# Both heads of a pair in one reduction over the partitions, pool sums behind it, and weights two column tiles ahead

## The chip, the cores and the metric

The kernel runs on one core of a Trainium2 chip. The metric is the device time of one execution in microseconds; of the kernel before, three runs are known: 1245.39, 1246.07 and 1249.59, median 1246.07. The engines of the core are TensorE (PE in the rows, with its weight loads as PEld), VectorE (DVE), ScalarE (ACT), GpSimd (POOL) and SyncE (SP), which here issues every transfer. Each engine works through its own queue in order and waits at the head of it until what it needs is there.

## The reference

Two layers of an encoder on 1024 prompt tokens and 32 sample tokens, all in fp32, width 1024.

- Layer 0: RMSNorm, one input projection to 3072 columns, which are split into `u`, `q`, `k`, `v`, `g_pool`, `g_att` of 512 each. The pooling branch takes trailing means of `u` over windows of 2, 4, 8 and 16 tokens (one window for each group of 128 channels), subtracts the token, and maps each group by a 128x128 matrix. The attention branch has 8 heads of 64 channels; a query sees its own chunk of 64 tokens and the 8 chunks before it, with a learned bias by clipped distance, and a softmax over the keys:

```
s = where(key_chunk >= 0, q @ k.T * 64**-0.5 + bias, -inf)
p = softmax(s, axis=-1);  o = p @ v
```

  Both branches are multiplied by SiLU gates, concatenated, and go through an output projection, RMSNorm and a residual.
- Layer 1: RMSNorm, a projection to 5128 columns, an mLSTM mixer with 4 heads of 256 channels in chunks, gates, an output projection, RMSNorm and a residual. The change reaches it only through the number of buffers.

## The kernel before, in words

Activations lie transposed, channels on the partitions and the 1056 tokens along the free dimension, in three token groups of 384, 384 and 288. Each projection is computed in column tiles of 128. A weight tile is split into a rounded part `wh` and a residue `wl`, the activations likewise, and three products give fp32 accuracy: per column tile and token group that is 24 matmuls (`mm3`, lines 107 to 109), called a dense step here. `load_w` fetches a weight tile in two halves into `wr` (two buffers), ScalarE casts them to `wh` (line 94), and VectorE or GpSimd subtracts to get `wl` (line 95). `wh` and `wl` have two buffers each, so the next tile is loaded while one is in use.

Layer 0 runs over four pairs of heads. Dense steps that belong to later work (a next `q`, `v`, `u` or gate tile, by the table PLAN) are put on a list, and `fill()` takes the next step from it wherever attention would leave TensorE without work; `fill_all()` takes the rest ahead of the next pair. `take()` hands out the loaded weight tile and starts the load of the next one.

Attention of a pair is done for each head `e` in two halves `hf` of 512 queries, keys on the partitions. `att_s` computes scores (lines 353 and 354: two matmuls for each key block, into `ps`), adds the bias while evacuating to `st` (VectorE at 363, ScalarE at 371), takes the elementwise maximum over the key blocks on VectorE into `mx` (380 to 387), and lets GpSimd take the maximum over the partitions into `mb` (389). `power` subtracts `mb` (396, VectorE) and takes the exponential (397, ScalarE). `att_pv` multiplies by the values (407), `att_take` copies the result out of PSUM into `ro` and `rg` (415, 416), and `att_out` divides (429, 430, VectorE), multiplies by the gate (431, GpSimd) and stores. `st` has four buffers; a head's first half takes one of them, its second half two. `ro`, `rg` and the PSUM tile `pv` have one buffer each. The order for a pair is: scores of both first halves, two fills, exponentials of head 0, scores of head 0's second half, a fill, exponentials of head 1, values of the first halves, scores of head 1's second half, values of head 0's second half, the sample's values (`values`, line 484), two fills with head 1's exponentials between them, values of head 1's second half. Each `att_s` issues a reduction of its own; the sample has a small one (464).

The pooling branch: once the last step of a `u` tile is through, `pool_sums` adds shifted copies on GpSimd (line 512: one addition for window 2, up to four for window 16). `finish` (519, 521, VectorE) is put on a list `due` and runs two fills later; the pooling matmul `pool_mix` (534) runs right after the gate tile's last step.

`out_proj` reads the mixed activations back through `xr` (two buffers) and projects them; the evacuation of its tiles is at lines 759 to 763.

The code fixes the order of the program, but the engines' queues are put in order by a planner that simulates a timeline ahead of the run (`schedule_with_timeline_sim=True`): an instruction that it deems ready can come ahead of an earlier one that it deems not ready. `issue_after(x)` keeps an instruction behind `x` on its engine.

Of the kernel before, what the change touches and what calls it, by code (L numbers as in the profile page):

```python
# [33 lines left out]
class Net:  # L34
# [43 lines left out]
    def load_w(self, src, keep=None, eng=None, parts=False):  # L78
        nc = self.nc
        eng = eng or nc.vector  # L80
        if isinstance(keep, tuple):
            wh, wl = keep
        elif keep is None:
            wh = self.wp.tile([128, 8, 128], F32R, name="wh")
            wl = self.wp.tile([128, 8, 128], F32R, name="wl")
        else:
            wh = self.lp.tile([128, 8, 128], F32R, name=f"wh{keep}")
            wl = self.lp.tile([128, 8, 128], F32R, name=f"wl{keep}")

        def part(i):  # L90
            k = slice(4 * i, 4 * i + 4)
            wr = self.wp.tile([128, 4, 128], F32, name="wr", bufs=2)
            self.wdma = nc.sync.dma_start(out=wr, in_=src[:, k]).ins
            nc.scalar.copy(out=wh[:, k], in_=wr)  # L94
            eng.tensor_tensor(out=wl[:, k], in0=wr, in1=wh[:, k].bitcast(F32), op=ALU.subtract)  # L95
        if parts:
            return (wh, wl), [lambda: part(0), lambda: part(1)]
        part(0)
        part(1)
        return wh, wl  # L100
# [229 lines left out]

    def att_s(self, pr, e, hf, Q, KA, KB, B):
        nc = self.nc
# [6 lines left out]
        for group in banks:  # L339
# [3 lines left out]
            for js in group:  # L343
# [32 lines left out]
                off += w  # L376
        mx = self.lp.tile([128, 512], F32, name="mx", bufs=2)
        if hf == 0:
# [6 lines left out]
        for j in rest:  # L385
            dst, a, b = place[j]
            nc.vector.tensor_tensor(out=mx[:, a - q0:b - q0], in0=mx[:, a - q0:b - q0], in1=dst, op=ALU.max)
        mb = self.lp.tile([128, 512], F32, name="mb", bufs=2)
        nc.gpsimd.partition_all_reduce(mb, mx, 128, bass_isa.ReduceOp.max)  # L389

# [109 lines left out]
    def pool_sums(self, g, u):  # L500
# [8 lines left out]
        while sh < w:  # L509
            dst = tmp[:, i % 2]  # L510
            lo += sh
            nc.gpsimd.tensor_tensor(out=dst[:, lo:L], in0=src[:, lo:L], in1=src[:, lo - sh:L - sh], op=ALU.add)
            src = dst
            sh *= 2
            i += 1

        def finish():
            with self.tc.issue_after(self.ev):
                nc.vector.tensor_tensor(out=src[:, 15:15 + w - 1], in0=src[:, 15:15 + w - 1], in1=self.cnt[:, g, :w - 1], op=ALU.mult)
                for a, n in ((15, SEQ), (30 + SEQ, DEC)):  # L520
                    nc.vector.scalar_tensor_tensor(out=u[:, a:a + n], in0=src[:, a:a + n], scalar=1.0 / w, in1=u[:, a:a + n],
                                                   op0=ALU.mult, op1=ALU.subtract)
        self.due.append([2, finish])

# [15 lines left out]
    def layer0(self):  # L540
# [13 lines left out]
        def take(want):  # L554
            assert seq[nxt[0]] == want
            if not self.wq:
                self.wq.append(self.load_w(w0[want]))
            nxt[0] += 1
            if nxt[0] < len(seq):
                self.wq.append(self.load_w(w0[seq[nxt[0]]], None, self.weng))  # L560
            return self.wq.pop(0)
# [102 lines left out]
        def do_gp(g):  # L664
            def make():
                pools["gp", g] = self.lq.tile([128, T], F32, name="gp", bufs=1)
                return self.gated(pools["gp", g])
            self.later(lambda: take(GP + g), xs, make, lambda: self.pool_mix(g, pools["u", g], pools["gp", g]))

        for pr in range(NPAIR):  # L670
# [19 lines left out]

            def S(e, hf):
                return self.att_s(pr, e, hf, Q, KA, KB, B)
            scores()
            p00, w00 = S(0, 0)
            p10, w10 = S(1, 0)
            self.fill(2)
            w00()
            p01, w01 = S(0, 1)
            self.fill()
            w10()  # L700
            power()
            od = self.att_new()
            self.att_pv(0, 0, p00, vt, od)
            self.fill()
            w01()
            self.att_pv(1, 0, p10, vt, od)
            self.att_out(pr, od, 0, 512, gate)
            p11, w11 = S(1, 1)
            self.fill()
            od = self.att_new()  # L710
            self.att_pv(0, 1, p01, vt, od)
            values()
            self.fill()
            w11()
            self.fill()
            turn()
            self.att_pv(1, 1, p11, vt, od)
# [8 lines left out]
    def out_proj(self, wsrc, gpost, late, resid, finish, ytiles=(), nx0=4, nopen=2, end=False, w2=2, anchor=None):  # L726
# [7 lines left out]
        for gi in range(3):  # L734
            s, n = GR[gi]
            x = self.new_x(gi)
            for k in early + list(late):
                if k in late:
                    src = late[k][:, s:s + n]
                else:  # L740
                    xr = self.tp.tile([128, 384], F32, name="xr", bufs=2)
                    with tc.issue_after(wdma) if gi and 1 else nullcontext():
                        nc.sync.dma_start(out=xr[:, :n], in_=mv[:, k, s:s + n])
                    src = xr[:, :n]
                with tc.issue_after(anchor) if gi and anchor is not None else nullcontext():
                    self.split_x(x, k, src, None, nc.gpsimd if gi < 2 and k % 2 == 0 else None)
# [71 lines left out]
    def gate_weights(self):  # L818
        nc, wp = self.nc, self.wp
        wr = wp.tile([128, 8, 64], F32, name="wr", bufs=2)  # L820
        nc.sync.dma_start(out=wr, in_=self.io["w1g"])
        wh = wp.tile([128, 8, 128], F32R, name="wh")
        nc.scalar.copy(out=wh[:, :, 0:64], in_=wr)
# [455 lines left out]
```

## Time and profile before

| | |
|---|---|
| median of three runs | 1246.07 us |
| the profiled execution's own time | 1249.51 us |
| its span | 1247.8 us |
| mean granted TensorE clock | 0.983 |
| busy: TensorE, weight loads | 1193.3 us (96%), 1143.3 us (92%) |
| busy: VectorE, ScalarE, GpSimd | 688.4 us, 473.6 us, 308.6 us |
| moved by DMA | 94.03 MB, mean 75 GB/s |

The span runs from the first to the last instruction; what lies around it is the difference to the execution's own time, 1.7 us. Layer 0's pairs lie between about 50 and 430 us, its output projection from there to about 570 us, layer 1 behind that. A granted clock of 1.00 is TensorE's full rate of 2.4 GHz, 0.50 the lower of its two levels, 1.2 GHz.

### The profile page before, as it was taken

Reading aid. Unit: us, or ns where it says so; the run is one execution under the profiler, and the core shown is the slowest. Engines: PE = TensorE matmul, PEld = TensorE weight load, DVE = VectorE, ACT = ScalarE, POOL = GpSimd, SP = SyncE. Lnnn points to the kernel's source line nnn. Section 1 sums busy time; section 2 is a strip of 40 time slices with the busy share of each in tenths; the row PEclk is TensorE's granted clock in tenths of the full one; section 3 lists DMA queues with packets and bytes.
Section 4 is the critical chain, followed back from the end, with each engine's and each line's share of the span. In section 5 each row is a group of like instructions: output and inputs, shape, how many; then the busy total and the mean of one; then the engine's idle time right before and its main releaser. Section 6 shows DMA issues by size and latency. Waiting matters only on the chain.

```text
span 1247.8 us, 19532 instructions
## 1 busy us (share of the span) xinstructions
PE 1193.3 (96%) x7457; PEld 1143.3 (92%) x7457; DVE 688.4 (55%) x1460; ACT 473.6 (38%) x980; POOL 308.6 (25%) x402
## 2 busy tenths in 40 slices
PE   7998899999997989999999999999999999999996
PEld 7997798897896889998999899999999999998996
DVE  7677457577476644675436533655247532566324
ACT  7542235344443364542134332443124322445421
POOL 1234322433224233551011210121003110123232
PEclk9999899999998999999999899999999999999998
DMA  8311220121210462331111321122111321114333
GB/s 252 95 35 35 71 61 26 39 83 36 88 35 26 125 192 71 105 120 56 59 36 43 83 76 44 47 70 82 51 34 53 77 86 35 43 61 140 113 101 127
DMA packets 79613, 94.03 MB, mean 75 GB/s; under 512 B 19208, under 2 KB 56856, under 8 KB 79520
## 3 DMA queue, kind: packets, MB, share of 16 engines
q1 hardware_dynamic: 79520, 92.79, 24.3%
q8 instruction: 58, 0.95, 0.3%
q14 instruction: 35, 0.29, 0.1%
HBM read 72.64 MB, written 21.69 MB: 76 GB/s over the span
## 4 chain that ended last, share of the span: by engine, by line
PE 54%; DVE 5%; DMA 5%; issue 2%; ACT 1%; POOL 1%; SPq 0%; DVEq 0%; ACTq 0%; POOLq 0%
PE pd L107 15%; PE pd L109 15%; PE pd L108 15%; DMA MA<-mdr 2%; PE pm L938 1%; DMA xr<-mix 1%; PE ps L1006 1%; DMA wr<-in_w0o 1%; PE pv L973 1%; PE pv L975 1%; PE pv L974 1%; PE ps L973 1%; DVE wl L95 1%; PE ps L975 1%; PE ps L974 1%
## 5 line engine op out<-in xcount | busy, mean ns | idle before, releaser
L107 PE MATMUL pd<-xh,wh 128*128 128x384 f32 (+1 forms) x1864 | 610.8, 328 | 10.9 <-ACT wh L94 6.3
L109 PE MATMUL pd<-xh,wl 128*128 128x384 f32 (+1 forms) x1864 | 612.2, 329 | 0.4 <-DVE wl L95 0.2
L108 PE MATMUL pd<-xl,wh 128*128 128x384 f32 (+1 forms) x1864 | 610.9, 328 | 1.6 <-DVE xl L208 0.9
L107 PEld LDWEIGHTS pd<-xh,wh 128*128 128x128 f32 x1864 | 354.6, 190 | 15.9 <-ACT wh L94 6.9
L108 PEld LDWEIGHTS pd<-xl,wh 128*128 128x128 f32 x1864 | 354.6, 190 | 4.6 <-DVE xl L208 1.3
L109 PEld LDWEIGHTS pd<-xh,wl 128*128 128x128 f32 x1864 | 354.9, 190 | 3.5 <-DVE wl L95 1.6
L94 ACT CAST wh<-wr 128x512 fp32r<-128x512 f32 x158 | 91.5, 617 | 128.3 <-PE pd L108 99.4
L95 DVE TENSOR_TENSOR wl<-wr,wh 128x512 fp32r<-128x512 f32 x116 | 79.3, 706 | 31.2 <-ACT wh L94 29.5
L95 POOL TENSOR_TENSOR wl<-wr,wh 128x512 fp32r<-128x512 f32 x42 | 58.8, 1414 | 112.5 <-ACT wh L94 69.3
L407 PE MATMUL pv<-st,vt 128*128 128x512 f32 (+1 forms) x192 | 59.2, 455 | 11.9 <-ACT st L397 11.9
L193 POOL TENSOR_TENSOR acc<-acc,sqt 128x384 f32<-128x384 f32 (+1 forms) x41 | 46.9, 1145 | 80.2 <-ACT sqt L192 80.0
L407 PEld LDWEIGHTS pv<-st,vt 128*128 128x128 f32 x192 | 36.2, 198 | 32.9 <-ACT st L397 12.8
L396 DVE TENSOR_TENSOR st<-st,mb 128x512 f32<-128x512 f32 (+1 forms) x96 | 41.0, 495 | 45.0 <-POOL mb L389 24.4
L74 POOL TENSOR_SCALAR_AFFINE_SELECT D<-D 128x128 f32<-128x128 f32 (+1 forms) x36 | 12.4, 345 | 180.2 <-ACT D L1002 167.3
L1018 POOL TENSOR_TENSOR qa<-qT,MA 128x128 f32<-128x128 f32 (+1 forms) x64 | 27.1, 441 | 108.4 <-DMA MA<-mdr 71.3
L262 DVE TENSOR_TENSOR row<-pd,r 128x384 f32<-128x384 f32 (+1 forms) x36 | 18.4, 521 | 63.4 <-PE pd L109 63.3
L1020 POOL TENSOR_TENSOR qal<-qa,qah 128x256 fp32r<-128x256 f32 (+1 forms) x32 | 27.3, 856 | 103.5 <-ACT qah L1019 92.5
L397 ACT ACTIVATE st<-st 128x1280 f32<-128x1280 f32 x24 | 30.5, 1271 | 55.5 <-DVE st L396 54.6
L371 ACT ACTIVATE st<-ps,far 128x256 f32<-128x256 f32 (+3 forms) x56 | 27.0, 486 | 57.1 <-DVE st L363 32.6
L1038 DVE SCALAR_TENSOR_TENSOR C<-C,MA,ps 128x258 f32<-128x258 f32 x64 | 30.4, 478 | 33.0 <-PE ps L975 18.8
L389 POOL PARTITION_ALL_REDUCE mb<-mx x16 | 29.1, 1823 | 49.1 <-issue 42.6
L264 DVE SCALAR_TENSOR_TENSOR kT<-pd,r 128x384 f32<-128x384 f32 (+1 forms) x24 | 12.6, 524 | 49.5 <-PE pd L109 49.3
(305 smaller groups left out, 1681.8 us busy)
## 6 DMA issues: line engine op xcount, KB each, us to landing
wr<-in_w SPq DMA_DIRECT2D x128, 256.0 KB, 2.8
xr<-mix SPq DMA_DIRECT2D x26, 192.0 KB, 3.1
wr<-in_w0o SPq DMA_DIRECT2D x16, 256.0 KB, 3.2
MA<-mdr SPq DMA_DIRECT2D x32, 128.0 KB, 3.2
wr<-in_w1o SPq DMA_DIRECT2D x16, 256.0 KB, 2.8
x<-in_x SPq DMA_DIRECT2D x16, 192.0 KB, 2.8
x<-x1d SPq DMA_DIRECT2D x16, 192.0 KB, 3.9
out_y<-y SPq DMA_DIRECT2D x16, 192.0 KB, 2.1
```

The costliest lines, as they stand in the source:

```text
L94: nc.scalar.copy(out=wh[:, k], in_=wr)
L95: eng.tensor_tensor(out=wl[:, k], in0=wr, in1=wh[:, k].bitcast(F32), op=ALU.subtract)
L107: nc.tensor.matmul(out=p, lhsT=wh[:, k], rhs=xh[:, k], start=first and i == 0, stop=False)
L108: nc.tensor.matmul(out=p, lhsT=wh[:, k], rhs=xl[:, k], start=False, stop=False)
L109: nc.tensor.matmul(out=p, lhsT=wl[:, k], rhs=xh[:, k], start=False, stop=last and i == len(ks) - 1)
L193: (eng or nc.gpsimd).tensor_tensor(out=acc, in0=acc, in1=t[:, :n], op=ALU.add)
L389: nc.gpsimd.partition_all_reduce(mb, mx, 128, bass_isa.ReduceOp.max)
L396: nc.vector.tensor_tensor(out=dst, in0=dst, in1=mb[:, a - q0:b - q0], op=ALU.subtract)
L397: nc.scalar.activation(out=st, in_=st, func=AF.Exp)
L407: nc.tensor.matmul(out=pv[:, a - q0:b - q0], lhsT=vt[:, j, 64 * e:64 * e + 128], rhs=dst, start=(i == 0), stop=(i == len(order) - 1))
L1020: nc.gpsimd.tensor_tensor(out=qp[1], in0=qa[:, :, :L], in1=qp[0].bitcast(F32), op=ALU.subtract)
L1038: nc.vector.scalar_tensor_tensor(out=Cn[:, d], in0=C[:, d], scalar=Ab[:, L - 1:L], in1=pu, op0=ALU.mult, op1=ALU.add)
```

## The change

The two heads of a pair share `mx` and `mb` of 2 x 512 columns (one buffer each), and one reduction of 1024 columns follows the scores of both. The second halves of both heads are scored together, after the values of the first halves. The sample's values and their transposition (`turn`) move ahead of the second halves' exponentials. The additions of `pool_sums` are issued behind the latest reduction (`self.par`), `finish` runs three fills later instead of two, and `pool_mix` is put on the same list, three fills later for groups 2 and 3 and without delay for groups 0 and 1. `take` loads until three tiles are on hand; `wh`, `wl` and `wr` have three buffers, `xr` has four, and the memory for this comes from a smaller scratch area for dynamic transfers.

```diff
@@ load_w, gate_weights: three buffers
-            wh = self.wp.tile([128, 8, 128], F32R, name="wh")
-            wl = self.wp.tile([128, 8, 128], F32R, name="wl")
+            wh = self.wp.tile([128, 8, 128], F32R, name="wh", bufs=3)
+            wl = self.wp.tile([128, 8, 128], F32R, name="wl", bufs=3)
...
-            wr = self.wp.tile([128, 4, 128], F32, name="wr", bufs=2)
+            wr = self.wp.tile([128, 4, 128], F32, name="wr", bufs=3)
@@ att_s
-    def att_s(self, pr, e, hf, Q, KA, KB, B):
+    def att_s(self, pr, e, hf, Q, KA, KB, B, mx, mb):
...
-        mx = self.lp.tile([128, 512], F32, name="mx", bufs=2)
+        mx, mb = mx[:, e], mb[:, e]
...
-        mb = self.lp.tile([128, 512], F32, name="mb", bufs=2)
-        nc.gpsimd.partition_all_reduce(mb, mx, 128, bass_isa.ReduceOp.max)
@@ pool_sums
-            nc.gpsimd.tensor_tensor(out=dst[:, lo:L], in0=src[:, lo:L], in1=src[:, lo - sh:L - sh], op=ALU.add)
+            with self.tc.issue_after(self.par):
+                nc.gpsimd.tensor_tensor(out=dst[:, lo:L], in0=src[:, lo:L], in1=src[:, lo - sh:L - sh], op=ALU.add)
...
-        self.due.append([2, finish])
+        self.due.append([3, finish])
@@ layer0, take
-            if not self.wq:
-                self.wq.append(self.load_w(w0[want]))
             nxt[0] += 1
-            if nxt[0] < len(seq):
-                self.wq.append(self.load_w(w0[seq[nxt[0]]], None, self.weng))
+
+            while len(self.wq) < 3 and nxt[0] - 1 + len(self.wq) < len(seq):
+                self.wq.append(self.load_w(w0[seq[nxt[0] - 1 + len(self.wq)]], None, self.weng if self.wq else None))
             return self.wq.pop(0)
@@ layer0, do_gp
-            self.later(lambda: take(GP + g), xs, make, lambda: self.pool_mix(g, pools["u", g], pools["gp", g]))
+            self.later(lambda: take(GP + g), xs, make,
+                       lambda: self.due.append([3 * (g > 1), lambda: self.pool_mix(g, pools["u", g], pools["gp", g])]))
@@ layer0, order of a pair
-            def S(e, hf):
-                return self.att_s(pr, e, hf, Q, KA, KB, B)
+
+            def S(hf):
+                mx = self.lp.tile([128, 2, 512], F32, name="mx", bufs=1)
+                mb = self.lp.tile([128, 2, 512], F32, name="mb", bufs=1)
+                res = [self.att_s(pr, e, hf, Q, KA, KB, B, mx, mb) for e in range(2)]
+                self.par = nc.gpsimd.partition_all_reduce(mb.rearrange("p e t -> p (e t)"), mx.rearrange("p e t -> p (e t)"), 128,
+                                                          bass_isa.ReduceOp.max).ins
+                return res
             scores()
-            p00, w00 = S(0, 0)
-            p10, w10 = S(1, 0)
+            (p00, w00), (p10, w10) = S(0)
             self.fill(2)
             w00()
-            p01, w01 = S(0, 1)
-            self.fill()
             w10()
             power()
+            self.fill()
             od = self.att_new()
             self.att_pv(0, 0, p00, vt, od)
             self.fill()
-            w01()
             self.att_pv(1, 0, p10, vt, od)
             self.att_out(pr, od, 0, 512, gate)
-            p11, w11 = S(1, 1)
+            (p01, w01), (p11, w11) = S(1)
+            values()
+            self.fill(2)
+            turn()
+            w01()
             self.fill()
+            w11()
             od = self.att_new()
             self.att_pv(0, 1, p01, vt, od)
-            values()
             self.fill()
-            w11()
-            self.fill()
-            turn()
             self.att_pv(1, 1, p11, vt, od)
             self.att_out(pr, od, 512, 1024, gate)
@@ out_proj
-                    xr = self.tp.tile([128, 384], F32, name="xr", bufs=2)
+                    xr = self.tp.tile([128, 384], F32, name="xr", bufs=4)
@@ kernel
-    nc = bacc.Bacc("TRN2", target_bir_lowering=False, num_devices=1)
+    nc = bacc.Bacc("TRN2", target_bir_lowering=False, num_devices=1, dynamic_dma_scratch_size=2048)
```

## Rows read from the trace of the kernel before

**Rows 1.** The page's first part: busy us (share of the span) and instructions.
```profile
PE 1193.3 (96%) x7457; PEld 1143.3 (92%) x7457; DVE 688.4 (55%) x1460; ACT 473.6 (38%) x980; POOL 308.6 (25%) x402
```
**Rows 2.** Waits of TensorE: line, what released it: us, times, longest.
```profile
PE pv L407 <- ACT st L397: 11.9, 4, 6.3
...
PE pv L484 <- ACT rg L416: 5.8, 2, 3.8
PE pd L107 <- ACT qT L763: 3.9, 1, 3.9
PE pm L534 <- DVE u L521: 3.9, 1, 3.9
```
**Rows 3.** Windows: us; busy PE, PEld, DVE, ACT, POOL; granted clock, DMA share, GB/s.
```profile
550.00:575.00 25.00, 21.92 (x140) 21.16 (x139) 18.98 (x46) 9.59 (x22) 8.39 (x9) 1.00 0.32 103
1125.00:1175.00 50.00, 45.86 (x259) 41.57 (x258) 28.16 (x59) 29.39 (x62) 16.46 (x14) 1.00 0.48 152
1175.00:1200.00 25.00, 25.00 (x149) 25.00 (x149) 9.07 (x20) 6.37 (x14) 9.84 (x6) 1.00 0.27 87
```
**Rows 4.** Windows behind two of the waits, the granted clock before the last two numbers.
```profile
119.50:123.90 4.40, 4.40 (x30) 3.87 (x31) 1.28 (x4) 0.46 (x1) 1.80 (x1) 0.61 0.00 0
138.50:144.40 5.90, 5.85 (x17) 5.25 (x18) 4.63 (x7) 0.00 (x0) 0.00 (x0) 0.51 0.47 126
```
**Rows 5.** Timeline of GpSimd, pair 0: start, us, instruction [idle before <- what ended it].
```profile
74.20 0.54 POOL L464 PARTITION_ALL_REDUCE smb<-sm  x1 [6.33 <-DVE mx L380]
74.66 1.87 POOL L389 PARTITION_ALL_REDUCE mb<-mx  x1
...
96.21 1.80 POOL L389 PARTITION_ALL_REDUCE mb<-mx  x1 [6.29 <-issue]
...
105.07 3.52 POOL L95 TENSOR_TENSOR wl<-wr,wh 128x512 fp32r<-128x512 f32 x2 [6.92 <-issue]
...
130.43 1.98 POOL L512 TENSOR_TENSOR qT<-qT 128x1079 f32<-128x1079 f32 x1 [7.28 <-issue]
```
**Rows 6.** Timeline of VectorE, pair 0.
```profile
98.05 3.31 DVE L396 TENSOR_TENSOR st<-st,mb 128x128 f32<-128x128 f32 x8 [6.48 <-POOL st L375]
101.27 3.36 DVE L429 RECIPROCAL rg<-rg 128x256 f32<-128x256 f32 x2
...
134.97 1.22 DVE L519 TENSOR_TENSOR qT<-qT,cnt 128x15 f32<-128x15 f32 x1 [7.49 <-POOL qT L512]
```
**Rows 7.** Groups of instructions, 50 to 430 us: busy us, mean ns | idle before, releasers.
```profile
L387 DVE TENSOR_TENSOR mx<-mx,st 128x256 f32<-128x256 f32 (+2 forms) x64 | 38.2, 606 | 1.2
...
L397 ACT ACTIVATE st<-st 128x1280 f32<-128x1280 f32 x24 | 30.5, 1271 | 55.5 <-DVE st L396 54.6 <-DVE srec L487 0.8
...
L363 DVE TENSOR_TENSOR st<-ps,B 128x256 f32<-128x256 f32 (+1 forms) x72 | 24.7, 370 | 16.8 <-PE ps L354 16.5
...
L431 POOL TENSOR_TENSOR ro<-ro,ga 128x512 f32<-128x512 f32 x8 | 12.3, 1532 | 26.4 <-ACT th L277 8.7 <-issue 6.7 <-DVE ro L430 6.0
...
L415 ACT COPY ro<-pv 64x512 f32<-64x512 f32 x16 | 9.2, 578 | 29.0 <-PE pv L407 21.3 <-DMA mix<-ro 7.7
...
L383 DVE TENSOR_TENSOR mx<-st 128x512 f32<-128x512 f32 x8 | 7.3, 908 | 0.0
...
L484 PE MATMUL pv<-vt,ss 128*32 128x65 f32 (+1 forms) x80 | 7.1, 234 | 5.8 <-ACT rg L416 5.8
```
**Rows 8.** Window over four score matmul pairs of 1280 columns in all.
```profile
70.53:71.91 1.38, 1.38 (x10) 1.30 (x10) 1.31 (x4) 0.02 (x1) 0.00 (x0) 1.00 0.00 0
```
**Rows 9.** Timeline of TensorE, pair 0: values of two heads.
```profile
101.16 2.42 PE L407 MATMUL pv<-st,vt 128*128 128x512 f32 x8 [0.91 <-ACT st L397]
...
103.60 2.32 PE L407 MATMUL pv<-st,vt 128*128 128x512 f32 x8
```
**Rows 10.** The chain that ended last, 434 to 452 us: start, us, what.
```profile
435.27 4.02 DMA wr<-in_w0o
...
440.69 3.93 DMA wr<-in_w0o
```

More of the change, by code (lines that the diff above doesn't have):

```diff
@@ L819, in gate_weights @@
         nc, wp = self.nc, self.wp
-        wr = wp.tile([128, 8, 64], F32, name="wr", bufs=2)
+        wr = wp.tile([128, 8, 64], F32, name="wr", bufs=3)
         nc.sync.dma_start(out=wr, in_=self.io["w1g"])
-        wh = wp.tile([128, 8, 128], F32R, name="wh")
+        wh = wp.tile([128, 8, 128], F32R, name="wh", bufs=3)
         nc.scalar.copy(out=wh[:, :, 0:64], in_=wr)
```

## The prediction

> **What bounds the kernel now.** I read the busy shares first. TensorE is busy for 1193.3 us of a span of 1247.8 [rows 1], so no other engine can be what sets the total; what can be won is the 54.5 us in which it does no work, and the time in which it works at a lower clock. The page's matmul ends are modelled, so 54.5 is rough. The Trainium skill ("Perfetto Trace Analysis", section "Identifying the Most-Contended Engine") warns that matmul occupancy is a poor measure of what is left and asks for the weight loads' share instead; by it 1247.8 - 1143.3 = 104.5 us would be open and the ceiling would be twice as high. I don't take it as a ceiling here, since loads stand still whenever a matmul streams longer than its load takes, as those of line 407 do.
>
> Then the waits of TensorE [rows 2]. Four of them make up 25.5 us, all in layer 0 or at its end: 11.9 us in four waits of the value matmuls (L407) for the exponentials; 5.8 us in two waits of the sample's value matmuls (L484); 3.9 us of the pooling matmul (L534) for the pooled rows; 3.9 us at the first output projection for an evacuation (L763). Small ones lie where stages meet: 3.1 us in 550:575, and 4.1 us in 1125:1175 [rows 3].
>
> Third, the clock. Behind these waits the granted clock falls to about half: in 119.5:123.9 it is 0.61 while TensorE is busy for the whole 4.4 us, so 1.7 us are lost; in 138.5:144.4 it is 0.51, and 2.9 us are lost [rows 4]. There are five of the first size (behind both L484 waits, behind L407 at 300 and 393, behind L763 at 451) and one of the second (behind L534): 5 x 1.7 + 2.9 = 11.4 us, so a wait costs nearly one and a half times its length.
>
> Last, why the waits exist. GpSimd's timeline [rows 5] shows partition reductions of 0.54 us (64 columns) and 1.8 to 1.9 us (512 columns), but in front of one that follows ordinary work lie some 6 us that nothing in the profile explains ("issue", 6.29), and behind it, before the next ordinary tensor instruction, as much again (6.92 and 7.28). So a change of kind costs about 6.2 us on the way in and 7.1 on the way out, while a second reduction right behind the first pays neither. Each pair of heads has three groups of reductions before, hence three round trips of some 13 us. Three of the four waits hang on them: L407 waits through subtraction and exponential for a reduction that came late; the pool sums were cut in two by a reduction, and VectorE then stood 7.49 us in front of L519 [rows 6]; and L484 waits for a buffer that ScalarE empties only when `ro` is free, which needs GpSimd's product L431 and its store (L415 waits 7.7 us for that store [rows 7]).
>
> **The change part by part.** The sum is made against the profiled execution, 1249.5 us, which is 3.4 above the median of the runs shown; I put the base midway, at 1247.8.
>
> *One reduction for both heads.* Per pair three groups of reductions become two, so one round trip of 13.3 us goes per pair, 53 us of GpSimd time in all, none of it on TensorE directly. The Trainium skill ("GPSIMD Engine Reference", section 2.1) says that the first call into a freshly loaded kernel pays about 6 us with nothing visible in the profile; the row in front agrees (6.29). It names no price for the way back, where rows 5 show 6.92 and 7.28; by the page alone 4 x 6 = 24 us of GpSimd time would go, work behind a reduction would start 7 us sooner than I assume, and rival 2 would lose its ground and its 0.16 to the forecast. The reduction of 1024 columns is in no row. Below it can't cost less than one of 512 (1.8), above not more than two (3.7); between 64 and 512 columns it grows by 1.3 us per 448, which carried on gives 3.2, and that I take.
>
> *First half.* The joint reduction can start only when head 1's maxima are there, and ends some 3.2 us later than head 0's did. Program order has three dense steps between scores and values there, and the planner places others; I cost it at nothing, at most 0.6 us per pair if its order stays as it is.
>
> *Second half: the new critical piece.* Before, head 0's second half was scored, reduced and exponentiated while the first half's values still ran. Now both heads' second halves start behind them. VectorE's chain from there: reciprocals 3.4 [rows 6] and two products (1.2, at a max's length); per head five bias additions at 0.37, one copy-maximum at 0.91 and six maxima at 0.61 [rows 7], 6.4, so 12.8 for two heads; two dense evacuations, estimated near a max's length, 0.5 each: 18.4 us. Then the reduction (3.2), half of one head's subtractions (3.31 / 2 [rows 6]) and one exponential (1.27 [rows 7]): 24.5 us until head 0's values can start. TensorE has beside it: the scores, 1.4 us per 1280 columns [rows 8], 2560 per head, so 5.6 for both; the sample's values, 7.1 / 4 = 1.8 [rows 7]; three dense steps of 24 matmuls at 25.00 / 149 = 0.168 [rows 3], 4.0 each, 12.1: 19.5 us. It lacks 5.0 us. Order in the program isn't order on the engine: at 101.16 and 103.60 two heads' values stand with nothing but one dense matmul between them [rows 9], though the program has a whole dense step there, so the planner pulls forward what it deems ready. One more step of 4.0 us pulled in leaves 1.0 us; with the planner's error I take 1.4 per pair, 5.6 in all, and the clock falling behind two of the four, 2 x 1.7 = 3.4. Cost: 9.0 us. Bounds: 0 when two steps are pulled in; 5.0 + 1.7 per pair, 27, when none is.
>
> *The way in of that second reduction* is hidden if GpSimd's last ordinary instruction ends 6.2 us before the maxima are ready. That is L431 of the first half, whose inputs are ready some 4.6 us into the chain of 18.4; it takes 1.5 [rows 7] and leaves 12. So I cost it at nothing; if the weights' residue (L95) slips in behind it, 6.2 us per pair appear.
>
> *What it takes off L407.* Late reductions were what it waited for; the chain above replaces them. I let half of 11.9 + 2 x 1.7 = 15.3 go, 7.7, and the 9.0 above is the rest's new price.
>
> *Sample values ahead of head 0's second half.* L484 needs the one value buffer in PSUM, which is now released by the first half's evacuation, long done. 5.8 + 2 x 1.7 = 9.2 us go. What is late next is the sample's own exponential, issued a whole step earlier: nothing.
>
> *Pool sums behind the reduction, finish a step later, mix up to two steps later.* The sums are no longer cut by a change of kind, but always start behind one: 7.1 us, then up to four additions of 2 us and a tile's residues, some 18 us after the reduction. The mix now comes two dense steps and the second half's values later. 3.9 + 2.9 = 6.8 us go. On GpSimd the residues of weights queue behind the sums; being two tiles ahead (a tile is three dense steps, 12 us) covers that. If the cover is missing, the price is rival 2.
>
> *Weights two ahead, three buffers; four `xr` buffers.* In steady state TensorE waits for weights for almost nothing, so the extra tile is worth nothing there: below nothing would need more transfers, and there are none. At the output projection the transfers come in pairs, 5.4 us from one to the next of a buffer (435.27 to 440.69 [rows 10]), so a weight tile of two halves arrives per 5.4 us where a step uses it in 4.0; three buffers give 3.6. ScalarE's evacuation L763 stands behind such a cast. Of 3.9 + 1.7 = 5.6 I let 4.6 go. Of the 7.2 us where stages meet [rows 3], a third, 2.4. SP's queue gets the same transfers, only sooner. The smaller scratch for dynamic transfers touches none of the queues in the page.
>
> Sum: 9.2 + 6.8 + 7.7 + 4.6 + 2.4 = 30.7 won, 9.0 lost, net 21.7: 1247.8 - 21.7 = **1226 us**.
>
> **The rivals.**
> 1. *Everything goes.* Two steps are pulled in per pair and the planner's new order fits: 25.5 + 11.4 + 7.2 = 44.1, 1204 us. For it: all waits have one family of causes. Against: a planner that misjudges reductions once will do so again.
> 2. *Pool sums still hold VectorE.* They start 7 us later than an order without the way back expects, L519 stands at the head of VectorE as it did for 7.49 us, evacuations wait, and neither L534 (6.8) nor L407 (7.7) improves: 21.7 - 14.5 = 7.2 won, 1241 us.
> 3. *No cover.* No step is pulled into the second half: 27 us lost against 30.7 won, 1244 us; in effect, the waits move.
> 4. *Slower: the way in isn't hidden.* A residue L95 or the product L431 runs just ahead of the second reduction, which then comes 6.2 us late in every pair: 1.4 + 6.2 + 1.7 = 9.3 per pair, 37 against 30.7, 1254 us. It decides from 30.7 / 4 = 7.7 us per pair. For it: this is just what the reduction at 96.21 paid [rows 5]. Against: the chain is 12 us longer than L431 needs.
> That the change doesn't do what it says I find nowhere: fewer groups follow from the code.
>
> **How the numbers follow.** The forecast has 0.42 (its own range 1216 to 1236), rival 1 0.12, rival 2 0.16, rival 3 0.12, rival 4 0.18. Three tenths of a per cent, 3.7 us, is about what a measurement of this kernel tells from no change: faster means below 1242.3, slower above 1249.8. Rival 2 lies mostly below, rival 3 within, rival 4 above: faster 0.42 + 0.12 + 0.13 = 0.67, same 0.03 + 0.10 = 0.13, slower 0.20 with the worse side of rival 3. The range 1210 to 1250 leaves out most of rival 1's and of rival 4's chance, some 0.19.
>
> **What would show it.** Right: eight joint reductions of about 3.2 us, in the second halves with GpSimd waiting for the maxima and not for "issue"; no wait of L484; no cut in the pool sums; L407 waits of about 1 to 2 us in each pair; the granted clock full in 119 to 145; at the projection the transfers in threes. Wrong: "issue" of 6 us ahead of each second-half reduction with L407 waiting behind it (rival 4), a long stand of VectorE before L519 (rival 2), or new waits in layer 1, which this sum leaves as it is.

## The result and the profile after

The changed kernel takes 1219.12 us (median of four runs, 1218.05 to 1220.54), the kernel before 1246.86 us beside it: a ratio of 0.9774 [0.9758, 0.9789], 27.7 us won. The forecast was 1226 in a range of 1210 to 1250. Its profiled execution took 1220.54 us with a span of 1218.8 and a mean granted clock of 0.986. Some lines move by a few numbers: the value matmuls are L405 (before L407), the sample's L482 (L484), the pooling matmul L533 (L534), the joint reduction L695 (L389), the gate product L429 (L431), the additions of the pool sums L511 (L512), the exponential L395 (L397), the projection's evacuation L766 (L763).

The busy shares after, which answer to [rows 1]:

```profile
PE 1187.0 (97%) x7457; PEld 1141.1 (94%) x7457; DVE 677.9 (56%) x1460; ACT 472.4 (39%) x980; POOL 301.7 (25%) x394
```

TensorE is busy 6.3 us less with the same 7457 matmuls, and its mean granted clock is 0.986 where it was 0.983; the span fell by 29.0, so the rest is idle time of TensorE that has gone. GpSimd has eight reductions fewer. The waits of TensorE after (line, what released it: us, times, longest), to set beside [rows 2]:

```profile
PE pd L107 <- ACT wh L94: 7.5, 2, 5.3
PE pv L976 <- ACT Sh L1013: 2.2, 1, 2.2
...
PE ps L450 <- POOL wl L95: 1.4, 1, 1.4
...
PE pv L405 <- ACT rg L414: 1.0, 1, 1.0
```

The four rows on which the prediction rested are gone but for two rests: 1.0 us of the 11.9 of the value matmuls, and 2.2 at the output projection (the smaller wait in the first row; its 5.3 is the kernel's start). The largest rows left lie outside the pairs. Windows after (us; busy PE, PEld, DVE, ACT, POOL; granted clock, DMA share, GB/s):

```profile
119.00:144.50 25.50, 25.50 (x136) 22.38 (x135) 10.14 (x22) 9.67 (x14) 16.50 (x9) 1.00 0.13 42
...
50.00:62.00 12.00, 8.73 (x37) 8.11 (x35) 9.19 (x13) 8.25 (x14) 1.28 (x2) 0.72 0.37 112
415.00:423.50 8.50, 6.28 (x28) 5.68 (x27) 3.48 (x8) 3.69 (x8) 2.29 (x2) 0.80 0.61 179
...
523.00:548.00 25.00, 23.78 (x155) 23.15 (x154) 20.74 (x49) 11.50 (x26) 8.43 (x9) 1.00 0.35 113
1100.00:1150.00 50.00, 46.61 (x265) 44.87 (x265) 25.03 (x54) 26.99 (x59) 16.20 (x15) 0.97 0.33 105
668.00:700.00 32.00, 29.25 (x170) 27.32 (x169) 16.69 (x50) 9.21 (x25) 10.34 (x19) 0.84 0.26 60
```

The first row holds the place of both stretches of [rows 4]: TensorE is busy all through at the full clock. The others are where time is still lost; two of them are new losses, and they come up again below. GpSimd's timeline after, pairs 0 and 1 (start, us, instruction [idle before <- what ended it]):

```profile
78.77 0.55 POOL L462 PARTITION_ALL_REDUCE smb<-sm  x1 [6.00 <-DVE mx L380]
81.64 3.38 POOL L695 PARTITION_ALL_REDUCE mb<-mx  x1 [2.33 <-DVE mx L387]
...
110.65 1.28 POOL L429 TENSOR_TENSOR ro<-ro,ga 128x512 f32<-128x512 f32 x1
113.75 0.20 POOL L683 MEMSET B<- 64x128 f32 x1 [1.82 <-DMA B<-extr]
119.84 3.24 POOL L695 PARTITION_ALL_REDUCE mb<-mx  x1 [5.89 <-DMA mix<-smo]
130.22 1.99 POOL L511 TENSOR_TENSOR qT<-u 128x1085 f32<-128x1085 f32 x1 [7.13 <-issue]
...
206.60 1.29 POOL L429 TENSOR_TENSOR ro<-ro,ga 128x512 f32<-128x512 f32 x1 [0.33 <-DVE srec L485]
208.89 0.20 POOL L683 MEMSET B<- 64x128 f32 x1 [1.00 <-DMA B<-extr]
214.90 3.24 POOL L695 PARTITION_ALL_REDUCE mb<-mx  x1 [5.80 <-issue]
225.11 1.99 POOL L511 TENSOR_TENSOR qT<-u 128x1085 f32<-128x1085 f32 x1 [6.97 <-issue]
```

There is no reduction between the two halves any more (in [rows 5] one stands at 96.21), so two changes of kind to and fro are left per pair. The prediction says that nothing in the profile explains the idle time at such a change. The trace does have a row for it: two instructions MODIFY_POOL_CONFIG stand on GpSimd's queue at each change, in both directions. Those ahead of the large reductions, before and after (count: ns lowest/median/highest, first and last start):

```profile
L389 POOLq MODIFY_POOL_CONFIG  x16: 1/4/8, 90.1 to 404.3; - x16
...
L695 POOLq MODIFY_POOL_CONFIG  x8: 4/4/10, 114.1 to 378.3; - x8
```

Over all lines of the pairs there are 48 before (24 of them ahead of a reduction, 24 ahead of ordinary work) and 32 after (16 and 16), so 12 round trips have become 8. They take some ns themselves; the first of the second row, at 114.1, follows the end of a memset, and the reduction starts 5.7 us behind it.

The way in of the second halves is not hidden, though. VectorE's timeline in pair 1:

```profile
210.27 1.52 DVE L387 TENSOR_TENSOR mx<-mx,st 128x128 f32<-128x128 f32 x4
...
218.17 1.36 DVE L394 TENSOR_TENSOR st<-st,mb 128x128 f32<-128x128 f32 x3 [4.36 <-POOL mb L695]
```

The maxima are ready at 211.79, but a memset for the next pair's bias, which waits for a transfer, ended at 209.09, and the reduction starts 5.8 us behind that, at 214.90: 3.1 us late. In pair 0 the same arithmetic gives 2.7 us. Why no time is lost by it is told behind the experiments.

### The profile page after: what moved, and what is told of

It reads as the page before. It is cut to its first block, busy times and chain, and to the rows that moved or that the text cites. A ratio compares the mean times of both kernels' runs of the same rounds, so it can differ in the third digit from the quotient of the medians.

```text
span 1218.8 us, 19521 instructions
## 1 busy us (share of the span) xinstructions
PE 1187.0 (97%) x7457; PEld 1141.1 (94%) x7457; DVE 677.9 (56%) x1460; ACT 472.4 (39%) x980; POOL 301.7 (25%) x394
## 4 chain that ended last, share of the span: by engine, by line
PE 95%; ACT 1%; DMA 1%; DVE 1%; issue 1%; POOL 1%; SPq 0%; DVEq 0%; POOLq 0%; ACTq 0%
PE pd L107 25%; PE pd L109 25%; PE pd L108 25%; PE pv L405 4%; PE ps L353 1%; PE pm L941 1%; PE ps L354 1%; PE ps L1009 1%; PE pv L976 1%; PE pv L978 1%; PE pv L977 1%; PE ps L976 1%; PE ps L978 1%; PE ps L977 1%; PE pm L175 1%
## 5 line engine op out<-in xcount | busy, mean ns | idle before, releaser
L109 PE MATMUL pd<-xh,wl 128*128 128x384 f32 (+1 forms) x1864 | 607.9, 326 | 0.0
L109 PEld LDWEIGHTS pd<-xh,wl 128*128 128x128 f32 x1864 | 352.8, 189 | 2.2 <-DVE wl L95 0.5
L94 ACT CAST wh<-wr 128x512 fp32r<-128x512 f32 x158 | 91.4, 618 | 155.6 <-PE pd L108 109.9
L95 POOL TENSOR_TENSOR wl<-wr,wh 128x512 fp32r<-128x512 f32 x42 | 55.4, 1335 | 82.0 <-ACT wh L94 47.1
L405 PE MATMUL pv<-st,vt 128*128 128x512 f32 (+1 forms) x192 | 55.1, 433 | 1.0 <-ACT rg L414 1.0
L405 PEld LDWEIGHTS pv<-st,vt 128*128 128x128 f32 x192 | 35.0, 189 | 20.4 <-issue 11.0
L363 DVE TENSOR_TENSOR st<-ps,B 128x256 f32<-128x256 f32 (+1 forms) x72 | 25.3, 372 | 26.3 <-PE ps L354 25.9
L192 ACT ACTIVATE sqt<-pd 128x384 f32<-128x384 f32 (+1 forms) x40 | 18.3, 460 | 51.5 <-PE pd L109 51.5
```

The source lines that it names most:

```text
L109: nc.tensor.matmul(out=p, lhsT=wl[:, k], rhs=xh[:, k], start=False, stop=last and i == len(ks) - 1)
L405: nc.tensor.matmul(out=pv[:, a - q0:b - q0], lhsT=vt[:, j, 64 * e:64 * e + 128], rhs=dst, start=(i == 0), stop=(i == len(order) - 1))
```

## The experiments

The theory: the waits of before came from GpSimd's changes of kind, some 6 us into a partition reduction and some 7 us back to ordinary tensor work; a late reduction holds VectorE, then ScalarE's exponential, then TensorE. The change wins by keeping the reductions of two heads together. Rivals: the order of the program, the handling of the pool sums or the buffers do it.

**Two free reductions in place of the joint one**, all else as changed:

```diff
-                self.par = nc.gpsimd.partition_all_reduce(mb.rearrange(...), mx.rearrange(...), 128, bass_isa.ReduceOp.max).ins
+                for e in range(2):
+                    self.par = nc.gpsimd.partition_all_reduce(mb[:, e], mx[:, e], 128, bass_isa.ReduceOp.max).ins
```

> The changed kernel with two reductions of 512 columns, one directly behind the other, in place of the joint one of 1024; order of the heads, pool sums and buffers as changed. Theory (the order and the grouping carry the gain, the single instruction doesn't): two reductions behind one another pay one way in, 2 x 1.8 = 3.6 us against 3.24, so 1219 us, at most 4 us away. Rival (the joint instruction itself carries it, because the planner slips an ordinary GpSimd instruction between the two): some 6 us per group more, waits of the value matmuls in each pair, 1230 us or more.

1239.83 us against 1247.19, ratio 0.9943 [0.9919, 0.9966]: three quarters of the gain are gone. GpSimd in pair 0:

```profile
107.85 1.80 POOL L696 PARTITION_ALL_REDUCE mb<-mx  x1 [5.81 <-PE ps L354]
117.01 1.28 POOL L429 TENSOR_TENSOR ro<-ro,ga 128x512 f32<-128x512 f32 x1 [7.21 <-DVE mx L387]
118.25 2.88 POOL L95 TENSOR_TENSOR wl<-wr,wh 128x512 fp32r<-128x512 f32 x2
...
127.66 1.80 POOL L696 PARTITION_ALL_REDUCE mb<-mx  x1 [5.79 <-issue]
```

The planner put a gate product and two residues between the two reductions, and both ways are paid again: the second ends 19.8 us after the first. So it is in pair 1, with the two at 219.35 and 235.43; in pairs 2 and 3 the two start some 2 and 3 us apart. In all there are 10 round trips, with 40 MODIFY_POOL_CONFIG. TensorE's waits, one in pair 1 and one in pair 0, show who pays:

```profile
PE pv L405 <- ACT rg L414: 6.2, 1, 6.2
PE pv L405 <- issue: 4.0, 1, 4.0
```

**Two reductions, the second held right behind the first** (head 1's first, since its maxima are the last):

```diff
-                self.par = nc.gpsimd.partition_all_reduce(mb.rearrange(...), mx.rearrange(...), 128, bass_isa.ReduceOp.max).ins
+                first = nc.gpsimd.partition_all_reduce(mb[:, 1], mx[:, 1], 128, bass_isa.ReduceOp.max).ins
+                with tc.issue_after(first):
+                    self.par = nc.gpsimd.partition_all_reduce(mb[:, 0], mx[:, 0], 128, bass_isa.ReduceOp.max).ins
```

> The changed kernel with two reductions of 512 columns, head 1's first and head 0's held behind it on GpSimd, so that both are ready at once and nothing can come between. Theory (what the joint instruction buys is that no ordinary instruction splits a group): one way in and one way out per group, the pair of reductions takes 3.6 in place of 3.24 us, 1219 to 1223 us. Rival (one instruction is what matters, for instance because the planner lays out the whole kernel differently around two): 1232 us or more, as with the two that were free.

1219.02 us against 1246.96, ratio 0.9773 [0.9749, 0.9797], the whole gain. GpSimd, pair 0:

```profile
120.79 1.80 POOL L695 PARTITION_ALL_REDUCE mb<-mx  x1 [5.91 <-issue]
122.51 1.87 POOL L697 PARTITION_ALL_REDUCE mb<-mx  x1
```

Only the first pays the way in, and with 32 MODIFY_POOL_CONFIG the round trips are 8, as in the changed kernel. So it is not the single instruction that wins; it is that nothing ordinary stands between the two.

**The old order with a reduction per head**, pool sums and buffers as changed:

```diff
-            (p00, w00), (p10, w10) = S(0)
+            p00, w00 = S(0, 0)
+            p10, w10 = S(1, 0)
...
```

> The changed kernel with the old order of a pair and one reduction for each head and half; pool sums behind the latest reduction, three weight buffers and four xr buffers as changed. Theory (joint reductions and order carry most): the waits of the value matmuls (11.9 + 3.5 us with the clock) and of the sample's values (5.8 + 3.4 us) come back, 1243 us (1238 to 1248). Rival (the deeper buffers carry it, by freeing ScalarE's queue): 1219 to 1225 us.

1248.64 us, ratio 1.0011 [0.9992, 1.003]: no gain at all and just above the expected range, where the theory allowed a few us. TensorE waits as before, and more for the pool sums:

```profile
PE pv L407 <- ACT st L397: 8.9, 4, 3.0
PE pm L535 <- DVE u L522: 8.1, 2, 4.9
```

**The order and the joint reductions alone**, put into the kernel before (buffers, pool sums and due times as they were):

```diff
+                self.par = nc.gpsimd.partition_all_reduce(mb.rearrange(...), mx.rearrange(...), 128, bass_isa.ReduceOp.max).ins
...
-            p00, w00 = S(0, 0)
-            p10, w10 = S(1, 0)
+            (p00, w00), (p10, w10) = S(0)
```

> The kernel before with the joint reductions and the new order of a pair alone; pool sums, weight buffers and xr buffers as before. Theory (the joint reduction and its order carry nearly all): 1219 to 1226 us, the pool sums' old handling and the buffers being worth 3 us at most. Rival (the parts need one another: without the tile in hand, weights come late to the steps pulled in, or the sums split a group): 1232 us or more.

1223.57 us, ratio 0.9805 [0.9777, 0.9834]: 23.4 of the 27.9 us that two adjacent reductions win beside the same runs of the kernel before. The next two take parts of the rest out of the changed kernel.

**Pool sums, `finish` and `pool_mix` as before:**

```diff
-            with self.tc.issue_after(self.par):
-                nc.gpsimd.tensor_tensor(out=dst[:, lo:L], ...)
+            nc.gpsimd.tensor_tensor(out=dst[:, lo:L], ...)
...
-        self.due.append([3, finish])
+        self.due.append([2, finish])
```

> The changed kernel with the pooling branch as before: additions free to go ahead of a reduction, the finish two steps later, the pooling matmul right behind the gate tile. Theory (as priced in the prediction): the additions are cut or the finish stands in front of VectorE's queue, a wait of the pooling matmul of some 4 us and the clock behind it come back, 1226 us (1222 to 1230). Rival (with fewer changes of kind the sums find their place by themselves): 1219 us, at most 2 us away.

1222.13 us, ratio 0.9808 [0.978, 0.9836]: at most some 3 us, and the interval overlaps that of the change. The wait of the pooling matmul (L532 here) that the theory wanted back is 0.9 us, where the kernel before has 3.9.

**Weights one tile ahead in two buffers**, `xr` left at four:

```diff
-            wh = self.wp.tile([128, 8, 128], F32R, name="wh", bufs=3)
+            wh = self.wp.tile([128, 8, 128], F32R, name="wh")
...
-            while len(self.wq) < 3 and nxt[0] - 1 + len(self.wq) < len(seq):
+            if nxt[0] < len(seq):
```

> The changed kernel with two buffers for weights and one tile ahead; order, reductions, pool sums and four xr buffers as changed. Theory (buffers matter only where stages meet): the projection's wait grows from 2.2 to 3.9 us, the start of pair 0, where three tiles are now loaded at once, may get back up to 5 us: 1217 to 1223 us. Rival (the weights two ahead are what lets the planner pull in dense steps under the second halves): waits of the value matmuls come back, 1230 us or more.

1219.66 us, ratio 0.9784 [0.9748, 0.9821]: the third buffer is worth nothing that can be measured. One window says more, the start of pair 0, with two buffers:

```profile
50.00:62.00 12.00, 10.53 (x68) 10.39 (x67) 9.25 (x13) 7.61 (x14) 3.10 (x2) 1.00 0.32 90
```

The kernel before:

```profile
50.00:62.00 12.00, 10.53 (x68) 10.39 (x67) 9.71 (x13) 7.76 (x13) 3.10 (x2) 1.00 0.29 90
```

The changed kernel has 8.73 us of work there at a clock of 0.72. So loading two tiles ahead costs 1.8 us of waiting and 12 x 0.28 = 3.4 us of clock at this place, 5.2 in all in this execution; the total doesn't improve without it, and small waits appear elsewhere (2.1 us of L533, with the clock at 0.87 behind it in 400 to 410 us, and 1.4 of L109). The extra tile is not the only way to such a loss: the run without ordinary GpSimd work, below, has two buffers and 9.33 us of work there at 0.72.

**No ordinary GpSimd work in the attention of the kernel before**: residues of weights, gate products and pool sums go to VectorE; order, separate reductions and buffers stay.

```diff
-        nc.gpsimd.tensor_tensor(out=o[:, :n], in0=o[:, :n], in1=gate[:, q0:q1], op=ALU.mult)
+        nc.vector.tensor_tensor(out=o[:, :n], in0=o[:, :n], in1=gate[:, q0:q1], op=ALU.mult)
...
-        self.weng = nc.gpsimd
+        self.weng = nc.vector
```

> The kernel before with all of GpSimd's ordinary tensor instructions of the attention stage (weight residues, gate products, pool sums) moved to VectorE, so that during the pairs GpSimd runs only reductions and memsets and never changes kind. Order and separate reductions as before. Theory (late reductions are late through changes of kind): no wait of 6 us ahead of a reduction, waits of the value matmuls fall from 11.9 to under 3 us and those of the sample's values go; VectorE takes about 28 + 6 + 12 us more. 1225 to 1235 us. Rival (it is the order of the heads, not the changes of kind): waits stay, 1245 us or more.

1220.35 us, ratio 0.9781 [0.9756, 0.9806]: as good as the change, with the old order. The sixteen reductions there (ns lowest/median/highest):

```profile
L389 POOL PARTITION_ALL_REDUCE mb<-mx x16: 1784/1785/2613, 76.5 to 377.0; - x16
```

One of them in GpSimd's timeline:

```profile
94.92 1.78 POOL L389 PARTITION_ALL_REDUCE mb<-mx  x1 [1.30 <-DVE mx L387]
```

It answers to the one that stood at 96.21 behind 6.29 us of "issue" in [rows 5]; now it waits for its maxima only, and TensorE has none of the waits of [rows 2] at L407, L484 and L534. From 50 to 430 us one round trip is left, with 4 MODIFY_POOL_CONFIG; the memsets between the reductions bring none. This tells the theory from "it is the order": the old order is good once GpSimd doesn't change its kind. (It also takes load off GpSimd; the first experiment shows that with the same load the adjacency decides.)

**Both remedies at once**, the same three moves in the changed kernel:

```diff
-            with self.tc.issue_after(self.par):
-                nc.gpsimd.tensor_tensor(out=dst[:, lo:L], ...)
+            nc.vector.tensor_tensor(out=dst[:, lo:L], ...)
...
-        self.weng = nc.gpsimd
+        self.weng = nc.vector
```

> The changed kernel with GpSimd's ordinary tensor instructions of the attention stage moved to VectorE as well, so that there is nothing to change kind from. Theory (both cures remove the same waits): the attention stage has no waits left to lose, so no gain, 1217 to 1221 us. Rival (the changes of kind that the changed kernel still makes, some 3 us behind the maxima in the second halves, still cost): 1212 us or less.

1224.73 us, ratio 0.9818 [0.9791, 0.9846], beside the changed kernel run again in the same comparison as a control:

> The changed kernel itself, as the measure for the three beside it. 1219 us, at most 2 away.

1218.90 against 1247.58, ratio 0.9765 [0.9738, 0.9791]. The remedies don't add up, as the theory has it; that they cost some 6 us together it had not foreseen, and what that is stays open. The number of round trips alone is not what counts: here too one is left of the 8, and nothing more is won.

**The way in made late on purpose:** two additions of 16 columns that read the last maxima, right ahead of the second halves' joint reduction.

```diff
+                    nc.gpsimd.tensor_tensor(out=tr, in0=mx[:, 1, 496:512], in1=mx[:, 0, 496:512], op=ALU.add)
+                    ctx = self.tc.issue_after(nc.gpsimd.tensor_tensor(out=tr, in0=tr, in1=tr, op=ALU.add).ins)
```

> The changed kernel with two ordinary additions of 16 columns on GpSimd, dependent on the last maxima, directly ahead of the joint reduction of each second half, so that its way in can start only when the maxima are ready. Nothing is left out of the result. Theory (a change of kind costs some 6 us on the way in, which is now mostly hidden by GpSimd being free early): the second-half reductions come about 3 us later than in the changed kernel, where they already lay some 3 us behind the maxima; the value matmuls wait about as long in most pairs and the clock falls behind some: 4 x (3 + 1.7) = 19, so 1228 to 1240 us. Rival (dense steps pulled in cover it, since they stretch with the planner's order): 1219 to 1223 us.

1227.73 us, ratio 0.9844 [0.9819, 0.9869], 8.7 us above the run with two adjacent reductions beside it. GpSimd and TensorE in pair 1:

```profile
214.75 0.22 POOL L697 TENSOR_TENSOR tr<-mx 128x16 f32<-128x16 f32 x1 [2.82 <-DVE mx L387]
...
221.21 3.24 POOL L702 PARTITION_ALL_REDUCE mb<-mx  x1 [5.95 <-issue]
...
241.25 2.01 PE L405 MATMUL pv<-st,vt 128*128 128x512 f32 x3 [2.13 <-ACT rg L414]
```

The reduction starts 6.5 us behind the first addition, which waits for the last maxima; in the changed kernel it is 3.1 us behind them. Even so head 0's values, at 228.78, don't wait for it. The wait of 2.1 us is that of head 1's values, for the one value buffer in PSUM, which ScalarE has not emptied yet. The chain that ends there in the trace (start, us, what) comes by another path:

```profile
224.53 7.05 issue
231.59 1.99 POOL qT L511
233.57 1.25 POOL wl L95
...
234.84 2.49 DMA wr<-in_w
...
240.61 0.59 ACT rg L414
```

Behind the late reduction the way back, the first addition and a weight's residue come late too, and with the residue the buffer `wr` and the next transfer into it; ScalarE stands for this transfer with its cast (L94), ahead of the copies out of PSUM. In pair 0 the same stand costs 1.3 us; in pairs 2 and 3 the values wait for nothing. So the prediction's rival 4 has the lateness right, but neither the path, which was to be through the exponentials, nor the price: 8.7 / 4 = 2.2 us per pair for 6.5 us late in place of 3.1, where it reckoned 9.3.

**Layer 1, a fourth `MA` buffer** in the changed kernel, against its longest wait that is left (L976):

```diff
-            MA = lp.tile([128, 2, 128], F32, name="MA", bufs=3)
+            MA = lp.tile([128, 2, 128], F32, name="MA", bufs=4)
```

> The changed kernel with four buffers instead of three for the rows MA that layer 1's chunks read. The changed kernel waits 2.75 us at 675 us, where ScalarE stands for a transfer into MA, and works 10 us at about half the clock behind it (5 us). Theory (the transfer waits for its buffer): most of these 7.8 us go, 1211 to 1215 us. Rival (the transfer is late for its own length or another wait stands behind): 1217 to 1220 us.

1218.94 us, ratio 0.9767 [0.9741, 0.9793], no gain, as the rival has it. TensorE there:

```profile
675.98 0.39 PE L976 MATMUL ps<-Vh,wKh 128*128 128x258 f32 x1 [1.16 <-DVE C L1041]
...
677.24 0.38 PE L976 MATMUL ps<-Vh,wKh 128*128 128x258 f32 x1 [0.64 <-DVE S L1012]
...
678.94 0.58 PE L978 MATMUL pv<-Vh,Sl 128*128 128x258 f32 x1 [0.56 <-DVE Sl L1014]
```

The window over the waits' end and what follows:

```profile
678.00:689.00 11.00, 10.44 (x41) 9.35 (x39) 5.06 (x15) 2.00 (x5) 1.41 (x4) 0.53 0.55 131
```

In the changed kernel one wait of 2.24 us stands there, and its row for the same window is:

```profile
678.00:689.00 11.00, 10.43 (x39) 9.47 (x40) 4.65 (x14) 2.22 (x7) 2.17 (x5) 0.53 0.49 113
```

The wait has become several of 1.2 us and less, and the clock of the stretch is 0.53 in both.

**The same, and in pair 0 ScalarE's casts of the stacked `q` behind the copies of the value tokens**, against the wait at the start:

```diff
+            with tc.issue_after(self.vlast) if pr == 0 else nullcontext():
-            Q = self.stacked(qT, "qa")
+                Q = self.stacked(qT, "qa")
```

> The one before, and in pair 0 ScalarE's casts of the stacked q held behind the copies of the value tokens, on which the first dense steps wait. The changed kernel waits 3.3 us from 50 to 55 us and works 6.8 us at half the clock behind it (3.4 us). Theory (the casts of 2.1 us stand ahead of the copies): 2 to 4 us less than the one before, 1208 to 1213 us. Rival (another wait takes its place): no difference to the one before.

1216.63 us, ratio 0.9738 [0.9711, 0.9766]: 2.3 us below the control, but the intervals overlap, so it isn't told apart. Two of its six executions took 1211.10 and 1211.93 us at a mean clock of 0.994, the others 1216 to 1219 at 0.986 to 0.989. The window at the start, in one of the latter:

```profile
50.00:62.00 12.00, 10.24 (x45) 9.89 (x46) 9.80 (x14) 8.20 (x13) 0.79 (x1) 0.72 0.41 112
```

Of 3.3 us of waiting 1.8 remain; the clock is at 0.72, as in the changed kernel.

## Why the prediction was right, and where it was off

The direction and the mechanism were right: fewer changes of kind per pair, and with them the waits that hung on late reductions. By the prediction's terms, in us, measured on the two profiled executions (a stretch's loss of clock is its length times what the granted clock lacks to 1.00):

| term | forecast | measured |
|---|---|---|
| L484's waits and their clock | 9.2 | 9.2 |
| L534's wait and its clock | 6.8 | 6.8 |
| L407, less the new chain of the second halves | 7.7 - 9.0 = -1.3 | 15.3 - 1.0 = 14.3 |
| output projection | 4.6 | 5.6 - 2.2 - 8.5 x 0.20 = 1.7 |
| where stages meet | 2.4 | (3.1 - 1.2) + (4.1 - 3.4 - 50 x 0.03) = 1.1 |
| start of pair 0 | none | -5.2 |
| layer 1 behind 668 | none | about -2 |

Layer 1's row is the last window above, 2.75 us idle and 32 x 0.16 = 5.1 of clock, against 2.5 and 33 x 0.10 = 3.3 in 692 to 725 of before. All together makes 25.9 of the 29.0 us of span; the rest is spread over small waits and was not followed up. That the total came within 7 us of the forecast is in part luck: the third row is 15.6 us better than forecast, the four rows below it together 11.4 us worse.

*The step that failed: the cost of the second halves' new chain, in both of its terms.* The prediction let half of L407's wait go and then charged 9.0 us because TensorE had 19.5 us of work beside a chain of 24.5, with one dense step pulled in by the planner. From the end of head 1's first values to head 0's second values it takes 27.2 us in pair 0, but TensorE's own work fills that time; the chain is shorter. It was to start behind the first values, and the scores did not wait for them. Of the 16 score matmuls of line 353 that the second halves of a pair have, only five lie in this stretch (PE and PEld busy, as above):

```profile
103.90:131.13 27.23, 1.43 (x5) 0.76 (x4) 1.00 0.13 41
```

So the maxima, forecast 18.4 us into the chain, were ready after 13.2 us (at 117.11), in pair 1 after 12.3. Head 0's first exponential:

```profile
124.91 1.28 ACT L395 ACTIVATE st<-st 128x1280 f32<-128x1280 f32 x1 [1.32 <-DVE st L394]
...
219.97 1.28 ACT L395 ACTIVATE st<-st 128x1280 f32<-128x1280 f32 x1 [3.21 <-DVE st L394]
```

It ends 22.3 us into the stretch in pair 0 and 21.8 in pair 1, with the late reduction in it (2.7 and 3.1 us), where the forecast has 24.5 without. Head 0's values start at 131.13 and 225.70, 4.9 and 4.5 us behind this exponential and 2.2 and 2.9 behind head 0's second one.

The cover was missed too. Lines 107, 108 and 109 in the stretch of pair 0:

```profile
103.90:131.13 27.23, 15.97 (x49) 9.13 (x49) 1.00 0.13 41
103.90:131.13 27.23, 15.61 (x49) 9.20 (x49) 1.00 0.13 41
103.90:131.13 27.23, 15.49 (x48) 9.02 (x48) 1.00 0.13 41
```

146 matmuls are 6.1 dense steps of 24, where the order of the program has three there: the planner pulled in three, not one. In pair 1 it is 136, 5.7 steps. So TensorE has no gap in the first row of windows above, and its clock never falls there. The prediction's own bound ("0 when two steps are pulled in") was the case, and L407 gave back nearly all; the waits of 1 to 2 us in each pair that were named as a sign are one of 1.0 us in all. That is rival 1's reasoning, for these waits alone.

*"The way in is hidden" was wrong, and free.* The sign named for it, GpSimd waiting for the maxima and not for "issue", didn't come: the reduction is 2.7 and 3.1 us late in pairs 0 and 1. The prediction missed the memset of `B`, which waits for a transfer and ends 2.0 and 1.2 us behind the gate product L429. The rest is in its own terms: the product was to be done 12 us ahead of the maxima and ended 5.2 and 3.9 us ahead of them, less than the way in takes. TensorE doesn't pay, since the exponentials came in time even so.

*The projection was credited to the wrong edit.* Transfers do come in threes now, but the wait of 3.9 us at L763 has also left the run of order and joint reductions alone, which has two buffers as before and waits 1.7 us at this place, for a cast. The gain is smaller than forecast, since a wait of 2.2 us and a half-clock stretch remain at 417.

*The extra weight tile was not free.* "Below nothing would need more transfers" left out when they come: 5.2 us at the start of pair 0, which the run with two buffers doesn't lose.

*Pool sums: the right amount, credited to the wrong edit.* No reduction cuts them and L534 doesn't wait. But the old order with the new handling waits 8.1 us at that matmul, and the new order with the old handling 0.9 us (0.7 in the run of order and joint reductions alone), so it is the grouping that won most of these 6.8 us. The sign named for rival 2 did come: VectorE stands 15.4 us in four waits in front of `finish` (L518, L519 before), the longest of 8.0 us, against 19.7 us in three before. TensorE doesn't wait for it. The joint reduction takes 3.24 us, forecast 3.2.

## What to carry to other kernels

Where GpSimd serves both partition reductions and ordinary tensor work, look for MODIFY_POOL_CONFIG on its queue, and in its timeline for some 6 us ahead of a reduction and 7 us behind it in which nothing runs; group the reductions and hold them together by a dependence, or move the ordinary work off GpSimd, but expect only one of the two to pay. What a planner may slip between two instructions is part of an edit: two free reductions gave back three quarters of the gain that two adjacent ones keep. Before charging a longer chain to TensorE, count what independent work can be pulled into it, and which part of the chain can be done sooner, not only what the program's order puts there.

## What the runs showed of the hardware

- A change of kind costs GpSimd 5.8 to 6.3 us into a reduction and 6.9 to 7.3 us back in the rows shown of the changed kernel and the one before, with two MODIFY_POOL_CONFIG on its queue each time; a second reduction right behind a first one pays neither (two of 512 columns at 120.79 and 122.51), nor does one that has only memsets between it and the reduction before (in the run without ordinary work the one at 94.92 waits 1.30 us, for its maxima). The Trainium skill ("GPSIMD Engine Reference", section 2.1) gives about 6 us for a first call into a freshly loaded kernel, which the way in agrees with; for the way back, the larger part, it gives nothing.
- The joint reduction of 1024 columns takes 3.24 us, two of 512 columns 3.6 together: joining them saves next to nothing by itself.
- The loss of clock didn't follow the length of a wait: behind one of 2.24 us and behind three of 1.16, 0.64 and 0.56 us the granted clock of the same stretch was 0.53, and at the start of pair 0 it stayed at 0.72 when TensorE's waiting was cut from 3.3 to 1.8 us. With 8.73 us of work in the same 12 us it was 0.72 in the changed kernel and 0.86 in the run of two adjacent reductions.
